# Strided attention on one core: output stores of every second SBUF row, 16 KiB each, from pairs of groups

## The chip, the core and the metric

The kernel runs on one core of a Trainium2 chip. The metric is the device time of one execution in microseconds (us). Each run was timed beside the kernel before on the same chip. The profile's span (127.6 us for the kernel before) is a little shorter than the timed 129.3 us; inside the profile, times are us from the start of the span. A run counts as slow when it is over 1.5% above the fastest of the same kernel.

## The reference

Every query of 8 x 12 heads, 1024 positions and 64 dimensions attends to the 16 keys at positions 0, 64, 128, ... (stride 64).

```python
attend_positions = np.arange(0, seq, stride)
...
scores = np.einsum('bhqd,bhkd->bhqk', q, k) * scale
weights = np.exp(scores - np.max(scores, axis=-1, keepdims=True))
weights = weights / (np.sum(weights, axis=-1, keepdims=True) + 1e-10)
result[:, :, i, :] = np.einsum('bhqk,bhkd->bhqd', weights, v)[:, :, 0, :]
```

Q (25.2 MB) must be read and the output (25.2 MB) written; the keys and values used are small. All is float32 in HBM.

## The kernel before

It works on 24 groups of four heads. A group is 1 MiB of Q and 1 MiB of output; in SBUF it has 128 rows of 8 KiB. Each group goes through a cast to bf16 (GpSimd), a transpose (VectorE), score and output matmuls (TensorE), an exponential (ScalarE), and a normalisation that writes the output tile. All transfers are issued from one queue (SyncE).

```python
    QBUFS = 8
    OBUFS = 9
...
    def load(g):
        qn[g] = qn_pool.tile([P, 32 * D], FP32, name="qn", tag="qn")
        n = P if g < 2 else 32
        _copy(nc, qn[g], _ap_with(Q, [[HG * SD // n, n], [1, HG * SD // n]], g * HG * SD))
...
    def store(g):
        o = out_sb[g]
        _copy(
            nc,
            _ap_with(out, [[16 * D, P], [2 * SD, 2], [1, 16 * D]], g * HG * SD),
            _ap_with(o, [o.ap[0], [1, 1], [1, 32 * D]]),
        )
...
    for g in range(NG):
...
        store(g)
        if g + QBUFS < NG:
            load(g + QBUFS)
```

A load reads 32 runs of 32 KiB (the first two loads read 128 runs of 8 KiB). A store reads 128 SBUF rows of 8 KiB and writes each as two pieces of 4 KiB that lie 512 KiB apart in HBM; the pieces of neighbouring rows lie side by side, so that a store fills two solid blocks of 512 KiB.

The softmax here doesn't subtract the row's maximum and nothing guards it: scores larger than these inputs give would overflow.

## Time and profile before

| | before |
|---|---|
| time, median of the six runs beside the changed kernel | 129.38 us |
| moved by DMA | 51.12 MB on the queue |
| share of the 16 DMA engines' time | 96.7% |
| busiest compute engine | VectorE, 75% |
| compute hands over the last group | 119.86 us |
| last store landed | 126.05 us |

"Landed" means that the trace shows the transfer as complete, and "the line" is the transfers issued and not yet landed. The two figures that fix the end are the last two rows: how late the compute is done, and how long the line of transfers before the DMA engines is at that moment. The profile lines are shown in the prediction.

### The profile page before, as it was taken

The page shows a single profiled execution, that of the slowest core. Times are in us where ns is not written, and L with a number is a line of the kernel's source. Part 1 is how long each engine was busy: PE and PEld are TensorE (multiplying, and loading weights), DVE is VectorE, ACT ScalarE, POOL GpSimd, SP SyncE. Part 2 cuts the span into 40 slices and gives each one's busy share as a digit, 9 for nine tenths or more (in the row PEclk, how much of TensorE's full clock was granted, in tenths as well). Part 3 has the DMA queues.
Part 4 walks back from the last instruction along what each step waited for, and adds up shares of the span by engine and source line. Part 5 has one row for each costly group of instructions (what it writes and reads, how often), then busy time and mean ns, then how long its engine had stood idle before and what let it go on. Part 6 is the DMA issues. An engine that isn't in the chain of part 4 may idle for free.

```text
span 127.6 us, 1150 instructions
## 1 busy us (share of the span) xinstructions
PE 67.2 (53%) x292; PEld 30.1 (24%) x292; DVE 95.5 (75%) x167; ACT 57.5 (45%) x96; POOL 90.3 (71%) x89
## 2 busy tenths in 40 slices
PE   0005267766456796436757565379734877365100
PEld 0002032233222343212423232124221433132000
DVE  6947557788898678898879888897889878977300
ACT  4110614576771458776445653543554626462100
POOL 8962489877898286898888888898689887433300
PEclk9999999999955558999756999955999657998555
DMA  2999989898998998999989989999999999999980
GB/s 68 378 319 468 462 360 483 349 483 362 460 465 352 480 455 339 506 385 393 501 344 447 460 375 450 426 403 457 442 380 455 439 393 421 424 426 424 429 360 26
DMA packets 7910, 51.19 MB, mean 401 GB/s; under 512 B 3872, under 2 KB 3872, under 8 KB 3872
## 3 DMA queue, kind: packets, MB, share of 16 engines
q1 hardware_dynamic: 7904, 51.12, 96.7%
q8 instruction: 2, 0.03, 0.1%
q14 instruction: 4, 0.03, 0.1%
HBM read 25.95 MB, written 25.17 MB: 401 GB/s over the span
## 4 chain that ended last, share of the span: by engine, by line
DVE 48%; DMA 16%; PE 14%; issue 9%; POOL 4%; SPq 1%; ACT 0%; DVEq 0%; POOLq 0%
DVE out_sb L245 30%; PE o_ps L235 11%; DVE qt L203 10%; DMA out_dram<-out_sb 9%; DMA qn<-in_Q_dram 7%; DVE rec L243 7%; PE sc L210 3%; POOL out_sb L248 2%; POOL qb L199 1%; DVE v_rep L184 1%; SPq L35 1%; POOL v L191 1%; ACT out_sb L247 0%; SPq L100 0%; DVE k_r L159 0%
## 5 line engine op out<-in xcount | busy, mean ns | idle before, releaser
L235 PE MATMUL o_ps<-v,w 128*128 128x260 bf16 x192 | 40.0, 333 | 36.1 <-DVE out_sb L245 34.5
L221 ACT ACTIVATE w<-sc 64x512 bf16<-64x512 f32 x48 | 35.3, 735 | 30.1 <-PE sc L210 28.3
L199 POOL CAST qb<-qn 128x2048 bf16<-128x2048 f32 x24 | 45.3, 1889 | 4.2 <-DMA qn<-in_Q_dram 4.2
L245 DVE TENSOR_TENSOR out_sb<-o_ps,rec 128x768 f32<-128x768 f32 x48 | 46.0, 958 | 1.7
L248 POOL TENSOR_TENSOR out_sb<-out_sb,rec 128x512 f32<-128x512 f32 x24 | 25.0, 1042 | 22.2 <-ACT out_sb L247 22.2
L210 PE MATMUL sc<-qt,k_t 128*128 128x512 bf16 x96 | 33.3, 479 | 12.8 <-DVE qt L203 11.6
L235 PEld LDWEIGHTS <-w 128*128 128x128 bf16 x192 | 18.7, 113 | 63.5 <-DVE out_sb L245 48.1
L203 DVE STREAM_TRANSPOSE qt<-qb 128x1024 int32<-128x1024 int32 x24 | 29.6, 1233 | 4.7 <-POOL qb L199 4.7
L243 DVE RECIPROCAL rec<-o_ps 128x12 f32<-128x12 f32 (+1 forms) x72 | 15.3, 212 | 15.9 <-PE o_ps L235 15.8
L247 ACT COPY out_sb<-o_ps 128x512 f32<-128x512 f32 x24 | 14.0, 585 | 24.9 <-DVE rec L243 12.1
L191 POOL TENSOR_TENSOR v<-mask,v_rep 128x256 bf16<-128x256 bf16 x24 | 16.0, 669 | 2.3 <-DVE v_rep L184 2.3
L210 PEld LDWEIGHTS <-k_t 128*128 128x128 bf16 x96 | 10.8, 113 | 23.8 <-issue 10.7
L169 ACT COPY k_t<-k_r 32x128 bf16<-32x128 bf16 x20 | 5.9, 295 | 2.2 <-DVE k_r L159 1.9
L129 POOL MEMSET k_t<- 128x4608 bf16 x1 | 3.9, 3937 | 0.0
L180 PE MATMUL vp<-v_bf,perm_v 128*128 128x384 bf16 x4 | 1.8, 513 | 2.4 <-DVE v_rep L184 2.4
L139 DVE TENSOR_SCALAR s_sel<-col,slot_f 128x4 bf16<-128x4 int16 x1 | 2.5, 2546 | 0.1
L158 ACT CAST k_bf<-k_raw 128x256 bf16<-128x256 f32 x3 | 1.2, 405 | 3.1 <-DMA k_raw<-in_K_dram 3.0
L184 DVE CAST v_rep<-vp 128x384 bf16<-128x384 f32 x4 | 2.1, 543 | 0.6 <-PE vp L180 0.6
L123 DVE MEMSET k_t<- 128x1152 uint32 x1 | 1.0, 1018 | 1.0 <-PEq L311 1.0
L158 ACT ACT_TABLE_LOAD x1 | 1.3, 1283 | 0.7 <-PEq L311 0.7
L127 DVE MEMSET w<- 128x512 uint32 x3 | 1.5, 485 | 0.2
L118 POOL COPY perm_v<-identity 128x32 bf16<-128x32 bf16 x8 | 1.2, 209 | 0.0
(16 smaller groups left out, 5.0 us busy)
## 6 DMA issues: line engine op xcount, KB each, us to landing
qn<-in_Q_dram SPq DMA_DIRECT2D x24, 1024.0 KB, 11.7
out_dram<-out_sb SPq DMA_DIRECT2D x24, 1024.0 KB, 9.8
k_raw<-in_K_dram SPq DMA_DIRECT2D x1, 384.0 KB, 4.3
v_raw<-in_V_dram SPq DMA_DIRECT2D x1, 384.0 KB, 7.3
```

Source lines behind the costliest of these rows:

```text
L129: nc.gpsimd.memset(k_t[:, 8:NG], 0.0)
L169: op(k_t[dst : dst + 32, 8 * m + c : 8 * m + 8 : 2, :, col : col + NK], k_r[src : src + 32, 4 * m : 4 * m + 4].rearrange("p n (a k f) -> p ...
L191: nc.gpsimd.tensor_tensor(out=vb[g][:, 0 : 4 * D].rearrange("p (s d) -> p s d", s=4), in0=mask, in1=v_rep[:, g // 2, g % 2].unsqueeze(1).t ...
L199: nc.gpsimd.tensor_copy(out=qb[g], in_=qn[g])
L203: nc.vector.transpose(qt[g].bitcast(I32), qb[g].bitcast(I32))
L210: nc.tensor.matmul(sc, lhsT=k_t[:, g, f, NK * (1 - e) : NK * (1 - e) + P], rhs=_ap_with(q, [q.ap[0], [D, 8], [16 * D, 2], [2, 32]], extra_ ...
L221: nc.scalar.activation(out=_ap_with(wa, [wa.ap[0], [P, 8], [1, 2], [2, 32]], extra_offset=64 * a), in_=sc[64 * a : 64 * a + 64].rearrange( ...
L235: nc.tensor.matmul(ps[:, i, 0 : 4 * D + 4], lhsT=wt[g][:, i0 + i], rhs=vb[g], start=True, stop=True,)
L243: nc.vector.reciprocal(r, ps[:, 0:n, 4 * D : 4 * D + 4])
L245: nc.vector.tensor_tensor(out=to, in0=o, in1=by, op=ALU.mult)
L247: nc.scalar.copy(to, o)
L248: nc.gpsimd.tensor_tensor(out=to, in0=to, in1=by, op=ALU.mult)
```

## The change

The intent is fewer and larger packets for the stores: 64 packets of 16 KiB for 1 MiB instead of 128 of 8 KiB. To have 16 KiB in a row, two groups share one output tile (a pair). A store takes every second row of it (rows 0, 2, 4, ... or 1, 3, 5, ...), so that a transfer still has 1 MiB and still touches all parts of SBUF. Between two such half stores goes one load. Ten Q buffers and four output pairs replace eight and nine.

```diff
-    QBUFS = 8
-    OBUFS = 9
+    QBUFS = 10
+    OBUFS = 4
...
-            out_sb[g] = out_pool.tile([P, 4, 8, D], FP32, name="out_sb", tag="out_sb")
+            if g % 2 == 0:
+                out_2[g // 2] = out_pool.tile(
+                    [P, 2, 4, 8, D], FP32, name="out_sb", tag="out_sb"
+                )
+            out_sb[g] = out_2[g // 2][:, g % 2]
...
-    def store(g):
-        o = out_sb[g]
+    def store(n, h):
+        o = out_2[n][h : P : 2]
         _copy(
             nc,
-            _ap_with(out, [[16 * D, P], [2 * SD, 2], [1, 16 * D]], g * HG * SD),
-            _ap_with(o, [o.ap[0], [1, 1], [1, 32 * D]]),
+            _ap_with(
+                out, [[32 * D, 64], [2 * SD, 4], [1, 16 * D]],
+                2 * n * HG * SD + h * 16 * D,
+            ),
+            _ap_with(o, [o.ap[0], [1, 1], [1, 64 * D]]),
         )
...
-        store(g)
-        if g + QBUFS < NG:
-            load(g + QBUFS)
+        if g % 2 == 1:
+            for h in range(2):
+                store(g // 2, h)
+                if g - 1 + h + QBUFS < NG:
+                    load(g - 1 + h + QBUFS)
```

More of the change, by code (lines that the diff above doesn't have):

```diff
@@ L184, in value_rows @@
             nc.vector.tensor_copy(out=v_rep[:, 6 * n : 6 * n + 6, c], in_=vp)
-    qb, qt, wt, vb, rec, out_sb = {}, {}, {}, {}, {}, {}
+    qb, qt, wt, vb, rec, out_sb, out_2 = {}, {}, {}, {}, {}, {}, {}
     def values(g):
```

## The prediction

> **What bounds the kernel now.** I read, in turn, the page's busy shares and DMA digits, the DMA queue's own waits with the landings, and the end of the timeline. First the page: busy us by engine, then DMA share and rate in 40 slices of 3.19 us, then the queue's packets, MB and share of the 16 DMA engines.
>
> ```profile
> PE 67.2 (53%) x292; PEld 30.1 (24%) x292; DVE 95.5 (75%) x167; ACT 57.5 (45%) x96; POOL 90.3 (71%) x89
> ...
> DMA  2999989898998998999989989999999999999980
> GB/s 68 378 319 468 462 360 483 349 483 362 460 465 352 480 455 339 506 385 393 501 344 447 460 375 450 426 403 457 442 380 455 439 393 421 424 426 424 429 360 26
> ...
> q1 hardware_dynamic: 7904, 51.12, 96.7%
> ```
>
> No compute engine is near full, but the one queue that carries every load and store is busy for 96.7% of its 16 engines' time and falls off only in the last two slices. (The ripple in GB/s comes from packets of 32 KiB being counted at one moment.) So the DMA engines never run dry. How long the line before them is, the DMA issues of two short windows tell (one store each, issued at 92.61 us and, the last of all, at 119.86 us; the last column is us from issue to landing):
>
> ```profile
> out_dram<-out_sb SPq DMA_DIRECT2D x1, 1024.0 KB, 16.0
> ```
>
> ```profile
> out_dram<-out_sb SPq DMA_DIRECT2D x1, 1024.0 KB, 6.2
> ```
>
> The landings in the trace form a strict first-in-first-out train: from 11.8 us on something lands every 2.4 to 2.5 us, to the last store at 126.05 us. At 92.6 us six transfers stand in line; at the end one.
>
> The compute is almost as long. What the issuing queue waited for, over the whole span:
>
> ```profile
> SPq L35 <- DVE out_sb L245: 83.0, 24, 11.3
> ```
>
> All 24 stores wait for VectorE's last normalisation of their group, none for a DMA. In the queue's timeline the stores go out every 4.1 to 4.4 us in the long middle, and the timeline of all engines ends so (start, duration, what):
>
> ```profile
> 118.55 0.23 DVE L243 RECIPROCAL rec<-o_ps 128x12 f32<-128x12 f32 x1 [0.81 <-PE o_ps L235]
> 118.82 0.96 DVE L245 TENSOR_TENSOR out_sb<-o_ps,rec 128x768 f32<-128x768 f32 x1
> 119.86 0.54 SPq L35 DMA_DIRECT2D out_dram<-out_sb  x1
> ```
>
> So two bounds lie within a few us of each other: a DMA train that is full from start to end, and a compute loop that hands over its last group at 119.86 us, when only one other store is left in line. Does compute wait for loads? Of GpSimd's waits, the casts of Q waited 4.2 us in 3 pieces: the first two are the ramp (7.66 and 11.84 us), the third, 0.79 us at 106.27, is absorbed before VectorE needs the result at 109.20. So compute is not held by the train in the steady part.
>
> **What the Trainium skill says.** (1) "DMA: Bandwidth & Descriptors", section "Why a DMA increments its semaphore by 16 and not by 1": a DMA is split over the largest k up to 16 that divides the slowest dimension of both sides. 64 rows give k = 16, four rows per engine, so a half store still uses all engines. No trace yet shows it for 64 rows; the 128-row stores have 128 packets, 8 per engine. (2) "SBUF — State Buffer", section "Door 1: The DMA port swizzle": partitions 0 to 63 reach only 8 of the 16 ports and moved 196 GB/s against 328 for all 128. That is why the change takes every second row: both halves then touch all 16 ports. It is also the main danger: whether two DMA engines meet on one port at the same moment depends on how rows are dealt to engines, which neither page nor trace tells for this shape. (3) The first page's section "Anatomy of one DMA" puts a fixed cost of about 2 us on a transfer, mostly completion. Here it is smaller: the first packet ran at 1.84 us for an issue at 0.73 us (1.1 us), and the last packet ended at 125.60 for a landing at 126.05 us (0.45 us); I use these 1.55 us.
>
> **The change, part by part.**
>
> *Bigger packets.* The packet records have a median of 311 ns for 8 KiB (stores) and 1219 ns for 32 KiB (loads). A straight line through both has 8.3 ns fixed per packet and 0.0369 ns per byte, so 16 KiB should take 614 ns (estimate). A store of 1 MiB is now 8 x 311 = 2.49 us per engine (landings: 2.50 us after the one before) and becomes 4 x 614 = 2.455 us. Saved: 0.033 us x 24 = 0.8 us of a train of 124 us. A load, at 2.40 to 2.44 us, does not change. This is all that the intent can give, even if the train alone set the end.
>
> *Ten Q buffers.* Ten loads go out before the first store. In before, the eighth load landed at 26.68 us and two more transfers at 29.15 and 31.58 us; now these two are loads, and the first stores go out at 27.36 us (group 1's time in before). The line is not empty until 31.6 us, so no hole opens. Every later load lands some two store times (5 us) earlier; only the 0.79 us wait at 106.27 goes, which cost nothing.
>
> *Four output pairs.* Pair n+4 needs pair n's two stores landed. Carrying the train forward at 2.44 us a load and 2.46 us a half store, pair 0 lands at 39 us and is wanted at 56 (just after group 7's store at 54.95), pair 5 at 88 against 97, pair 6 at 98 against 106, pair 7 at 105 against 114. The nearest margin is some 8 us, so no wait. The build's order shows the compute engines' instructions in the same order and number. The issue order shows eight semaphores in turn, so at most eight transfers in flight; the deepest point of my train (four issues together at 79.9 us with five in line) holds the last load back by about 0.5 us and leaves no hole.
>
> *The pairing at the end.* Group 22's store, which went out at 116.59 us and had landed by 123.62, now waits for group 23: 2 MiB go out together at 119.86 us. The train before it ends where group 21 landed in before, 121.16 us, less 22 x 0.033 = 0.7, so at about 120.4 us. The last pair's first packet can run at 119.86 + 1.1 = 120.97 us, two halves take 2 x 2.455 = 4.91 us, and the landing adds 0.45 us: 126.33 us, against 126.05. That is +0.3 us. The queue has one hole of about 1 us at 120 to 121 us, and the 0.8 us saved vanishes in it.
>
> Sum: 129.3 + 0.3 = 129.6 us.
>
> **The rivals.** (a) *The train alone sets the end*: then the saving of 0.8 us shows, 128.5 us. For it: 96.7% busy. Against it: the compute's hand-over at 119.86 us does not move, and behind it lie 2 MiB. (b) *Half stores collide on SBUF ports, or 4 KiB pieces at every second address are slow in HBM*. Neither is seen in the trace. If all stores ran at half rate, 24 x 2.45 = 59 us come on top, about 188 us; a fifth slower on the stores, 24 x 0.5 = 12 us, about 141 us. Against it: loads already write 128 rows from 32 packets and run at full rate, and choosing every second row looks aimed at just this. I give it 15%. (c) *Bursts*: two stores and two loads every 8.2 us instead of one each every 4.1 us. If the line ran dry between bursts it would cost up to 1 us each; but by my train four or five transfers are in line at each burst until 97 us. Then it thins: two at 105.16, one at 113.46 us (group 21's hand-over, where the first packet at 114.6 us meets a line that is free at about 115). A hole there costs 0.5 to 1 us: 130.5 us.
>
> **Range and chances.** Expected 129.6 us. Without (b) I see 128.5 to 130.6 us; the upper end is widened a little for thin lines and a slightly slow 16 KiB packet: 128.6 to 131.2 us. 2% is 2.6 us, so faster needs under 126.7 us, which would need the compute to hand over earlier: 2%. Slower needs over 131.9 us, in practice (b): 16%. Within: 82%.
>
> **What would show each step.** Stores: 1536 packets of 16 KiB at a median near 614 ns, 6368 packets on the queue. The last VectorE instruction at 119.8 us within 0.5 us; the last two stores issued together just after; a dip of the DMA digits near 120 us; the queue's waits still all on VectorE. Wrong would be: 16 KiB packets well above 640 ns (rival b), compute waiting for output buffers or Q loads, or a last VectorE instruction that moves by over 1 us, which I have no reason for.

## More of the kernel before

One line more is needed for the comparison: the DMA view of the kernel before between 30 and 50 us (packets, MB, mean rate), a stretch in which stores and loads alternate.

```profile
DMA packets 776, 8.44 MB, mean 422 GB/s; under 512 B 131, under 2 KB 131, under 8 KB 131
```

## The result, and the profile after

The changed kernel takes 135.74 us (median of six; 134.43 to 136.58, one of them slow), against 129.38 us. The ratio is 1.0467, with a 95% interval of 1.0413 to 1.0521. (A ratio here is the mean time of one kernel's fast runs over that of the other's fast runs of the same rounds, so it is not quite the ratio of the medians.) It is slower, and outside the predicted range of 128.6 to 131.2 us.

The page of the changed kernel, the lines that answer to those shown of before:

```profile
PE 69.2 (52%) x292; PEld 30.9 (23%) x292; DVE 95.7 (72%) x167; ACT 57.6 (43%) x96; POOL 90.4 (68%) x89
...
DMA  3999999999999999999999999999999999999981
GB/s 74 363 334 476 403 471 393 393 471 275 368 307 383 319 388 354 373 395 395 383 437 403 403 442 408 422 437 403 432 422 422 412 437 417 422 442 408 422 354 74
...
q1 hardware_dynamic: 6368, 51.12, 96.6%
```

The compute engines did the same work in the same busy time (VectorE 95.7 against 95.5 us). The packets fell to 6368, as predicted. The DMA engines are as busy as before, 96.6%, but over a span that is 5.9 us longer. So they were not idle more; they worked more slowly. Where, the GB/s digits show: from the tenth slice (30 us) on they are at 275 to 395 for eleven slices, and only in the second half, from the 21st on, back at 400 to 440. In the same stretch of 30 to 50 us as above:

```profile
DMA packets 432, 6.81 MB, mean 340 GB/s; under 512 B 112, under 2 KB 112, under 8 KB 112
```

That is 340 GB/s instead of 422. Between 108 and 121 us, where only stores are left, the same view has no loss at all; first before, then after:

```profile
DMA packets 757, 5.53 MB, mean 425 GB/s; under 512 B 82, under 2 KB 82, under 8 KB 82
```

```profile
DMA packets 422, 5.55 MB, mean 427 GB/s; under 512 B 83, under 2 KB 83, under 8 KB 83
```

The trace's packet records put a number on each store. A 16 KiB packet has a median of 616 ns over the whole run, which is what the prediction had set as the check, but the mean is 676 ns: the median hides the slow ones. Between 30 and 50 us the mean is 860 ns and 44% take over 900 ns. Sorted by start and cut into quarters (of the 64 packets of a half store, so in the first store about each engine's first, second, third and fourth), the first half store has means of 622, 779, 1184 and 1131 ns: it starts at full rate and falls to half. Such stores become milder from one to the next and are gone by about 80 us. Over the run an engine spends 64.9 us in store packets, against 59.8 us before: 5.1 us more. The 32 KiB load packets add 0.5 us (44 per engine, on the mean 1242 instead of 1230 ns). Together that is most of the 6.4 us by which the last landing is later, 132.46 against 126.05 us.

The queue's waits changed as well:

```profile
SPq L35 <- DVE out_sb L249: 68.2, 11, 15.4
SPq L35 <- DMA qn<-in_Q_dram: 11.9, 8, 2.0
SPq L335 <- DMA out_dram<-out_sb: 9.0, 1, 9.0
SPq L35 <- DMA out_dram<-out_sb: 7.0, 4, 2.5
```

The issuing queue now waits 18.9 us, in 12 pieces, for transfers to land, because eight semaphores allow eight transfers in flight (the completions in this trace fall on eight) and the line had reached that. These waits cost nothing by themselves: the line was full while they lasted. The last loads came late, though: GpSimd's casts waited 6.9 us for Q, in 5 pieces, against 4.2 us in 3 before. The compute handed over 2.1 us later:

```profile
120.96 0.96 DVE L249 TENSOR_TENSOR out_sb<-o_ps,rec 128x768 f32<-128x768 f32 x1
121.98 1.37 SPq L35 DMA_DIRECT2D out_dram<-out_sb  x2
```

Even so it is not the hand-over that sets the end. The two stores issued at 121.98 and 122.56 us land at 130.00 and 132.46 us, 8.0 and 9.9 us later, because others stood before them. The DMA line sets the end, and it is longer since its stores were slow.

### The profile page after: what moved, and what is told of

It reads as the page before. It is cut to its first block, busy times and chain, and to the rows that moved or that the text cites. A ratio compares the mean times of both kernels' runs of the same rounds, so it can differ in the third digit from the quotient of the medians.

```text
span 133.5 us, 1125 instructions
## 1 busy us (share of the span) xinstructions
PE 69.2 (52%) x292; PEld 30.9 (23%) x292; DVE 95.7 (72%) x167; ACT 57.6 (43%) x96; POOL 90.4 (68%) x89
## 3 DMA queue, kind: packets, MB, share of 16 engines
q1 hardware_dynamic: 6368, 51.12, 96.6%
HBM read 25.95 MB, written 25.17 MB: 383 GB/s over the span
## 4 chain that ended last, share of the span: by engine, by line
DMA 51%; DVE 13%; POOL 12%; PE 7%; issue 5%; SPq 2%; ACT 0%; POOLq 0%; DVEq 0%
DMA qn<-in_Q_dram 51%; POOL qb L199 7%; DVE out_sb L249 7%; PE o_ps L239 4%; DVE qt L203 4%; PE sc L210 3%; POOL out_sb L252 2%; POOL v L191 2%; DVE rec L247 2%; SPq L35 1%; ACT out_sb L251 0%; SPq L100 0%; DVE v_rep L184 0%; SPq L98 0%; DVE k_r L159 0%
## 5 line engine op out<-in xcount | busy, mean ns | idle before, releaser
L239 PE MATMUL o_ps<-v,w 128*128 128x260 bf16 x192 | 40.8, 340 | 36.0 <-DVE out_sb L249 34.5
L210 PE MATMUL sc<-qt,k_t 128*128 128x512 bf16 x96 | 35.1, 501 | 13.1 <-DVE qt L203 11.6
L239 PEld LDWEIGHTS <-w 128*128 128x128 bf16 x192 | 19.2, 116 | 64.0 <-DVE out_sb L249 48.0
```

The source lines that it names most:

```text
L210: nc.tensor.matmul(sc, lhsT=k_t[:, g, f, NK * (1 - e) : NK * (1 - e) + P], rhs=_ap_with(q, [q.ap[0], [D, 8], [16 * D, 2], [2, 32]], extra_ ...
L239: nc.tensor.matmul(ps[:, i, 0 : 4 * D + 4], lhsT=wt[g][:, i0 + i], rhs=vb[g], start=True, stop=True,)
```

## The experiments

What had to be explained: why are the early half stores slow, at up to twice the time, why not in the beginning of each store, and why does it wear off? Two theories stood at the start. *Theory S*: every second row makes two DMA engines meet on one SBUF port. *Theory H*: it is the HBM side, every second 4 KiB. All experiments are edits of the changed kernel's `store`, unless said otherwise, and all keep its ten Q buffers and output pairs. Those with a wrong result send right rows to wrong places, or compute with stale Q.

### First call: which side of the store

**e1, full rows of one group, as before**

```diff
-        o = out_2[n][h : P : 2]
+        o = out_2[n][:, h]
-                out, [[32 * D, 64], [2 * SD, 4], [1, 16 * D]],
-                2 * n * HG * SD + h * 16 * D,
+                out, [[16 * D, P], [2 * SD, 2], [1, 16 * D]],
+                (2 * n + h) * HG * SD,
```

> The changed kernel with its pairing, its ten Q buffers, its four output pairs and its order of issues, but each store takes all 128 rows of one group, 8 KiB a row, as before. If the half store itself is slow (either of the two theories below), this is back at the time predicted from the order alone, 129 to 130.5 us, with 8 KiB packets at 311 ns. If the order and the bursts cost the 6.4 us, it stays at 134 to 136.5 us.

Measured: correct, 129.15 us (129.00 to 129.42), ratio 0.9982 (0.9951 to 1.0014). Packets at 311 ns throughout. So buffers and the pair tile are not the cause; the shape of the half store is. One weakness: here the first store of a pair can go out when its own group is done, so the run doesn't test two stores issued together. The next one does.

**e2, every second SBUF row, but HBM without holes** (wrong result)

```diff
-                out, [[32 * D, 64], [2 * SD, 4], [1, 16 * D]],
-                2 * n * HG * SD + h * 16 * D,
+                out, [[16 * D, 64], [SD, 4], [1, 16 * D]],
+                (2 * n + h) * HG * SD,
```

> Wrong result on purpose. SBUF side as in the changed kernel (every second row, 16 KiB), but a half store writes 1 MiB of HBM without holes: 4 KiB pieces of neighbouring rows lie side by side. Theory S (two DMA engines meet on one SBUF port because of every second row): still slow, 134 to 136.5 us, first 16 KiB packets of the early stores up to 1.2 us. Theory H (every second 4 KiB of HBM is slow to write): 129 to 130.5 us, all 16 KiB packets near 616 ns.

Measured: 130.14 us (129.61 to 130.80), ratio 1.0059 (1.0006 to 1.0112). Packets of 30 to 50 us have a mean of 642 ns, and only 4% take over 900 ns (in the last quarter of the very first store). This is what the prediction had in mind for the whole change, pairing at the end included.

**e3, full SBUF rows, but every second 4 KiB of HBM** (wrong result)

```diff
-        o = out_2[n][h : P : 2]
+        o = out_2[n][:, h]
-                out, [[32 * D, 64], [2 * SD, 4], [1, 16 * D]],
+                out, [[32 * D, P], [4 * SD, 2], [1, 16 * D]],
```

> Wrong result on purpose. HBM side of the changed kernel (each store fills every second 4 KiB of 2 MiB), SBUF side as before (128 rows of 8 KiB). Theory S: 129 to 130.5 us, packets at 311 ns. Theory H: slow, 134 us or more, 8 KiB packets well over 311 ns in the early stores.

Measured: 137.16 us (134.95 to 138.96; two of the four are slow, the two fast ones have 134.95 and 135.71). The profile, of a fast run, repeats the changed kernel's pattern with packets of half the size: the first store's quarters are 314, 372, 634 and 560 ns, and it wears off in the same way. Theory S is out: SBUF rows are those of before, and the slowness is all there. The three DMA views between 31.5 and 34 us, within the first half store, of the changed kernel, of e2 and of e3:

```profile
DMA packets 38, 0.62 MB, mean 249 GB/s; under 512 B 1, under 2 KB 1, under 8 KB 1
```

```profile
DMA packets 64, 1.05 MB, mean 419 GB/s; under 512 B 16, under 2 KB 16, under 8 KB 16
```

```profile
DMA packets 77, 0.65 MB, mean 259 GB/s; under 512 B 1, under 2 KB 1, under 8 KB 1
```

**e4, rows 0 to 63 and 64 to 127 as halves** (right result)

```diff
-        o = out_2[n][h : P : 2]
+        o = out_2[n][64 * h : 64 * h + 64]
-                2 * n * HG * SD + h * 16 * D,
+                2 * n * HG * SD + h * SD,
-                out, [[32 * D, 64], [2 * SD, 4], [1, 16 * D]],
+                out, [[16 * D, 64], [2 * SD, 4], [1, 16 * D]],
```

> Right result. A half store takes rows 0 to 63 or 64 to 127 instead of every second row; its HBM side has no holes between rows. Theory S with ports as the limit: half of the ports for each store, so stores take up to 4.9 us instead of 2.46 and the time goes to 150 to 190 us. Theory H: 129 to 130.5 us, as nothing lies at every second 4 KiB.

Measured: 141.56 us median of 135.70, 141.11, 142.02 and 142.04; the profiled run is a slow one (142.02), so I draw nothing from its size. Even the one fast run, 135.70 us, lies about 6 us above the kernel before. The time lies under what theory S expected and above theory H's.

### Second call: step, size of the holes, ports, packets

e3's slowness wears off, and in the records the engines drift apart while it does: in the changed kernel the share of time in which at least 13 of the 16 engines are in store packets falls from 52% (30 to 45 us) to 2% (75 to 90 us). In e1, which is never slow, it stays above 35% in both stretches. This suggested that the loss needs the engines in step.

**e6, half of the engines made to lag by one load before the first store** (right result)

```diff
     def load(g):
         qn[g] = qn_pool.tile([P, 32 * D], FP32, name="qn", tag="qn")
+        if g == QBUFS - 1:
+            for first, rows, k in ((0, 32, 8), (32, 32, 8), (64, 64, 16)):
+                _copy(
+                    nc, qn[g][first : first + rows],
+                    _ap_with(Q, [[rows * 32 * D // k, k], [1, rows * 32 * D // k]],
+                             g * HG * SD + first * 32 * D),
+                )
+            return
```

> Right result. The changed kernel, but the last load before the first store is split so that half of it (2 pieces of 8 shares) runs on 8 of the 16 DMA engines alone; these 8 then lag by about one load, 2.4 us, when the first half store starts. Theory H with relief by spread (a half store is slow only while nearly all 16 engines write the same half at once): the early 16 KiB packets run near 616 to 680 ns from the first store on, and the time is 130 to 132 us (the 129.6 of the order alone, plus about 1.2 us that the lagging engines end later). If the spread of the engines has nothing to do with it and something else wears off: early packets up to 1.2 us as before, 134 to 137 us.

Measured: correct, 131.25 us (131.07 to 131.40), ratio 1.0134 (1.0107 to 1.0160). For 75% of the time from 31 to 101 us eight engines store while eight load, give or take one (86% from 31 to 60 us). Only the first store still has a slow quarter (617, 862, 618, 616 ns); from the second on all quarters are at 611 to 639. Between 30 and 50 us the rate is back from 340 to 392 GB/s:

```profile
DMA packets 480, 7.84 MB, mean 392 GB/s; under 512 B 120, under 2 KB 120, under 8 KB 120
```

One load, cut differently, takes away most of the loss without touching a store. That step matters is thus shown, not inferred.

**e7, every second 8 KiB** and **e8, every second 16 KiB** (wrong results; e8 ran in the third call)

```diff
-        o = out_2[n][h : P : 2]
+        o = out_2[n][:, h]
-                out, [[32 * D, 64], [2 * SD, 4], [1, 16 * D]],
-                2 * n * HG * SD + h * 16 * D,
+                out, [[64 * D, P], [16 * D, 2], [1, 16 * D]],      # e7
+                2 * n * HG * SD + h * 32 * D,
+                out, [[128 * D, 64], [16 * D, 4], [1, 16 * D]],    # e8
+                2 * n * HG * SD + h * 64 * D,
```

> Wrong result on purpose. As the run with every second 4 KiB of HBM and 128 SBUF rows, but every second 8 KiB, still in pieces of 4 KiB. If it is the address bit of 4 KiB alone (half of something in HBM is then left out), both values occur now and it is fast: 129 to 130.5 us, 8 KiB packets at 311 ns. If any alternation does it: 134 us or more, early packets at up to 630 ns.

> Wrong result on purpose. As the run with every second 8 KiB, but every second 16 KiB (four pieces of 4 KiB side by side, then a hole of 16 KiB). If 4 KiB is the only size that matters: 129 to 130.5 us and 311 ns. If the address bit of 16 KiB selects something as well: 134 us or more.

Measured: e7 129.36 us (ratio 0.9990, 0.9964 to 1.0015), e8 129.14 us (0.9961, 0.9931 to 0.9991), packets at 311 ns in both. Holes of 8 or 16 KiB do no harm; holes of 4 KiB do.

**e9, rows 0 to 63 and 64 to 127, HBM without holes** (wrong result)

```diff
-        o = out_2[n][h : P : 2]
+        o = out_2[n][64 * h : 64 * h + 64]
-                out, [[32 * D, 64], [2 * SD, 4], [1, 16 * D]],
-                2 * n * HG * SD + h * 16 * D,
+                out, [[16 * D, 64], [SD, 4], [1, 16 * D]],
+                (2 * n + h) * HG * SD,
```

> Wrong result on purpose. SBUF side of the run with rows 0 to 63 and 64 to 127, HBM side without any holes (1 MiB in a piece). If that run was slow for its SBUF rows (half of the ports): 135 to 142 us again, and slow packets in the early and the last stores. If for its HBM side (every second 256 KiB): 129 to 130.5 us and 616 ns.

Measured: 138.23 us (137.09 to 140.62, the last a slow run), ratio 1.0644 (1.0600 to 1.0688), with a fast profile. The first store's quarters are 623, 718, 1082 and 1440 ns, and the last three stores are slow again (2.9 to 3.2 us per engine instead of 2.46). So e4's rows are a second, separate trouble, on the SBUF side, and the choice of every second row does avoid it. It, too, is mild while stores and loads overlap (612 to 690 ns in the quarters between 60 and 105 us), and the first three stores after the last load are at full rate as well (2.46 to 2.50 us per engine). Why the last ones are slow again is not shown.

**e5, one store of 2 MiB, all 128 rows of 16 KiB; the last pair as two stores** (right result)

```diff
-        o = out_2[n][h : P : 2]
+        if n < NC - 1:
+            if h == 1:
+                return
+            o = out_2[n]
+            _copy(nc, _ap_with(out, [[16 * D, P], [2 * SD, 4], [1, 16 * D]], 2 * n * HG * SD),
+                  _ap_with(o, [o.ap[0], [1, 1], [1, 64 * D]]))
+            return
+        o = out_2[n][:, h]
+        # then the store of e1
```

> Right result. The intent without the half stores: one store of 2 MiB takes all 128 rows of a pair, 16 KiB each; the last pair goes out as two stores of one group. Theory H: nothing is left out in HBM, so 16 KiB packets run at 614 to 616 ns throughout, the train is up to 0.8 us shorter, and the time is 128.5 to 130 us. If a 16 KiB packet is itself the trouble: 134 us or more.

Measured: correct, 129.85 us (129.20 to 130.92), ratio 1.0037 (0.9996 to 1.0079). In quarters of a store the 16 KiB packets run at 614 to 625 ns, except in the last quarter of the first store (730 ns). The packet size is not the trouble, and it is no gain either.

### Third to fifth call: what stands behind the store

**e10, even and odd places of 4 KiB mixed within a store** (wrong result; edit of e3)

```diff
-                out, [[32 * D, P], [4 * SD, 2], [1, 16 * D]],
+                out, [[32 * D, P], [4 * SD + (1 - 2 * h) * 16 * D, 2], [1, 16 * D]],
```

> Wrong result on purpose. The run with every second 4 KiB of HBM and 128 SBUF rows (134.95 us at best), with one thing changed: of a row's two 4 KiB pieces the first goes to an even place and the second to an odd one (the other way about in the other half). Row pitch, holes, piece size and packets stay. Theory H as the address bit of 4 KiB: both values occur in every store, so it is fast, 129 to 130.5 us, early 8 KiB packets near 311 ns. If the holes or the pitch of 8 KiB are what is slow: 134 us or more, early packets at up to 630 ns.

Measured: 153.94 us (152.38 to 155.93; two of the four are slow), which fits neither. The time has a dull cause: in this build the second store of a pair has a wait for the first one to land (12 waits for stores, 92.7 us in all). The packets are of more use. Every first store is at 309 to 315 ns, the very first included, where e3 had 634. But every second store of the mixed phase is slow in its second half (for example 329, 314, 410, 580 ns). So mixing even and odd places is not a full cure.

**e11, no load after the first ten** (wrong result)

```diff
                 if g - 1 + h + QBUFS < NG:
-                    load(g - 1 + h + QBUFS)
+                    qn[g - 1 + h + QBUFS] = qn[(g - 1 + h) % QBUFS]
```

> Wrong result on purpose. The changed kernel with its half stores, but no load after the first ten: later groups take the Q of an earlier one from SBUF. So stores have the DMA engines to themselves, and the engines start each pair of halves together after an idle stretch. If half stores are slow by their HBM addresses alone whenever all 16 engines write the same half together: packets of the later halves up to 1.2 us in every pair, to the end. If it takes loads from HBM beside the stores: all 16 KiB packets near 616 ns. The time is then the compute's, 127 to 131 us, and decides nothing.

Measured: 129.65 us (two runs). No packet is above 758 ns between 30 and 50 us, and the mean is 622, with the engines in step in every pair: 16 packets start within 0.14 to 0.16 us in nearly every store. The first half store of this kernel is the same instruction on the same data after the same ten loads as in the changed kernel. There it fell to 249 GB/s between 31.5 and 34 us; here the DMA view of the same stretch is:

```profile
DMA packets 80, 1.05 MB, mean 419 GB/s; under 512 B 16, under 2 KB 16, under 8 KB 16
```

The one difference is what stands in line behind it: a half store here, a load there. My theory H, that the addresses of the writes alone are slow, fell with this run.

**e12, every third 4 KiB of a 3 MiB region** (wrong result; edit of e3)

```diff
-                out, [[32 * D, P], [4 * SD, 2], [1, 16 * D]],
-                2 * n * HG * SD + h * 16 * D,
+                out, [[48 * D, P], [6 * SD, 2], [1, 16 * D]],
+                (2 * n + h) // 3 * 12 * SD + (2 * n + h) % 3 * 16 * D,
```

> Wrong result on purpose. 128 SBUF rows of 8 KiB; a store fills every third 4 KiB of 3 MiB instead of every second of 2 MiB (three groups share a region). There are more holes, but even and odd places of 4 KiB alternate from row to row. If what counts is that all pieces of a store have the same address bit of 4 KiB: fast, 129 to 130.5 us, early packets near 311 ns. If holes of 4 KiB as such are slow: 134 us or more, early packets at up to 630 ns.

Measured: 129.31 us (128.92 to 129.37), ratio 0.9978 (0.9932 to 1.0025), 311 ns. Holes of 8 KiB between single 4 KiB pieces do no harm where even and odd places alternate from row to row. Of all HBM patterns tried in a running line (e4 and e9, with their SBUF rows, aside), only those with every piece of the store at an even place, or every one at an odd place, were badly slow.

**e13, both half stores side by side, then both loads** (right result)

```diff
             for h in range(2):
                 store(g // 2, h)
-                if g - 1 + h + QBUFS < NG:
+            for h in range(2):
+                if g - 1 + h + QBUFS < NG:
                     load(g - 1 + h + QBUFS)
```

> Right result. The changed kernel with both half stores of a pair side by side and both loads after them. If a half store is slowed by a load directly behind it on all engines: first halves at 616 ns throughout, second halves of the early pairs up to 1.2 us a packet; about half of the 6.4 us is lost, 131.5 to 133.5 us. If loads anywhere in the mix do it: both halves slow, 134 to 137 us.

Measured: correct, 134.09 us (133.91 to 134.84), ratio 1.0357 (1.0316 to 1.0398). The time is a little above the range I gave, but the packets are as sharp as could be wished. The first halves of all pairs are at 615 to 622 ns (one quarter at 641). The second halves of the first four pairs have 1203, 1199, 1048 and 755 ns in their third quarter. In the changed kernel both halves have a load behind them and both are slow; here only the second half has one, and only the second half is slow. In the DMA views, first 31.5 to 34 us (mostly the first half), then 34 to 36.5 us (the second half, with a load behind it):

```profile
DMA packets 80, 1.05 MB, mean 419 GB/s; under 512 B 16, under 2 KB 16, under 8 KB 16
```

```profile
DMA packets 40, 0.66 MB, mean 262 GB/s; under 512 B 3, under 2 KB 3, under 8 KB 3
```

Less than half of the loss is saved (1.7 us of 6.4): fewer stores are slow, but the ones that are lose as much as before.

**e14, later loads copied from a tile in SBUF** (wrong result)

```diff
+    q_keep = const.tile([P, 32 * D], FP32, name="q_keep")
...
-                    load(g - 1 + h + QBUFS)
+                    sbuf_load(g - 1 + h + QBUFS)     # _copy(nc, qn[g], q_keep)
```

> Wrong result on purpose. The changed kernel with its order of halves and loads, but every load after the first ten copies 1 MiB from a tile in SBUF instead of HBM (that tile takes one load more at the start, about 2.4 us). If it is the load's HBM read that collides with the half store's HBM writes: 16 KiB packets near 616 ns from the first store on. If any transfer behind a half store does it, without HBM reads: early packets up to 1.2 us as in the changed kernel. The time decides nothing.

Measured: the early half stores stay at 612 to 643 ns; their mean between 30 and 50 us is 621. A transfer stands behind each of them, as in the changed kernel, but it does not read HBM (the run reads 12.32 MB of HBM, the changed kernel 25.95). So the mere presence of another transfer is not enough, and a read of HBM is what is missing. One more thing differs, though: the copy comes in 128 packets of 8 KiB where the load has 32 of 32 KiB, and no run separates the two. (The time, 134.1 us with one load more at the start, was not meant to decide.)

**e15, the two forms of e10 exchanged** and **e16, dense stores in e10's position** (wrong results; edits of e10 and of e1)

```diff
         o = out_2[n][:, h]
+        h = 1 - h                                     # e15
...
-                (2 * n + h) * HG * SD,
+                (2 * n + h) * HG * SD - h * 16 * D,   # e16: overlaps, so that it must wait
```

> Wrong result on purpose. The run with even and odd places mixed in each store, with the forms of the first and the second half exchanged; as there, the second half waits for the first to land, so the time is long (150 to 156 us) and decides nothing. If the slow packets there belonged to the place (second half, which starts after the queue ran dry, all engines in step): the second halves are slow again, and the first ones at 310 ns. If they belonged to the form (odd first, then even): now the first halves are slow and the second ones fast.

> Wrong result on purpose (the second store of a pair lies 4 KiB lower, so that it overlaps the first one's last piece and has to wait for it). Stores are those of before, 128 full rows and no holes, but the second one of a pair starts on an empty queue, all engines in step, with a load behind it, as in e10 and e15. If the place in HBM is a condition: 8 KiB packets near 311 ns in second stores too. If tight step and a load behind are enough: second stores of the early pairs slow in their second half, 400 to 620 ns, as in e10 and e15. The time is long in both cases, 145 to 156 us, by the wait.

Measured: e15 155.01 us, e16 153.09 us. In both, first stores have 309 to 315 ns and second stores are slow again (e15: 328, 314, 403, 596; e16: 328, 314, 448, 608 in the first pair, and 361 to 611 ns in the last quarter of the six after it). So the slowness in e10 went with the position, not with the form. And in this position even the dense stores of before are slow: the line before them has just run short (in e16 the engines stood idle for 0.07 to 0.93 us on the mean around the start of these stores), and a load is issued right behind. Tighter step alone does not tell them apart: in e16 their first 16 packets start within 0.32 us, but so do those of e8's first stores, in a running line with a load behind, at 311 to 315 ns. Late in these runs, where no loads are left, stores start within 0.14 to 0.31 us and are near full rate.

## Why the prediction was wrong

**What held.** The packet itself: 614 ns were estimated for 16 KiB and the median is 616. The 6368 packets, four per engine on all 16 engines for a half store, the compute engines' busy times, the order of issues, no hole after the first ten loads, and no wait of the compute for an output pair are all as predicted. The sum for the order and the pairing, 129.6 us, is close to e2's 130.14, which has the changed kernel's SBUF rows, pairing, order and packets, but no holes in HBM.

**The step that failed** is the one called "Bigger packets": "A store of 1 MiB ... becomes 4 x 614 = 2.455 us. Saved: 0.033 us x 24 = 0.8 us". The early stores took 3.7 us of each engine's time (622 + 779 + 1184 + 1131 ns), and all stores together cost 5.1 us more where 0.8 us less had been summed. I took a packet's duration from a trace in which stores were never in trouble and carried it over to a new pattern of addresses.

**A rival named the place and was dismissed for a wrong reason.** Rival (b) had "4 KiB pieces at every second address are slow in HBM" beside colliding SBUF ports, with 15%. Against it stood that loads run at full rate and that every second row looked aimed at avoiding ports. Both are arguments about SBUF; neither says anything about where the writes land. e2 and e3 each change one side only and show that the SBUF side is nearly innocent (e2) and the HBM side is enough (e3). The rival's size was off too, as it charged all 24 stores alike, while the loss wears off.

**What the runs showed in its place** are three conditions, each with a run that takes it away. (1) All pieces of the store lie at even, or all at odd, places of 4 KiB: without it, e2, e7, e8 and e12 are within 1% of before. (2) A load stands directly behind the store: without it, e11 has no slow stores (no quarter of one is over 665 ns), and in e13 only the halves with a load behind them are slow. That it is the load's read of HBM rests on e14 alone, whose copies also have smaller packets. (3) The 16 engines are in step: with half of them lagging, e6 gets back 4.5 us of the 6.4 (135.74 to 131.25). The third fits the wearing off: an engine that is held up falls behind the others, and so each slow store would spread the engines, until most of the time some write while others read. In the changed kernel the first 16 packets of a store start within 0.62 us in the first store and within 2.21 us in the sixth; that the slow stores cause this spread is inferred.

How can a load that comes later slow a store? The Trainium skill, "DMA: Bandwidth & Descriptors", section "Two DMAs through the same engine are not ordered", states that descriptors "*start* in order but are pipelined, and the engine's read and write sides are separate queues". Then the read side may already fetch the next load while the store's writes are still under way. This agrees with the slow packets being those of a store's second half, and with e11 and e13. That the reads run ahead is my inference; no record here shows a read apart from its write.

**The hand-over and the rival (a).** I had the compute's hand-over at 119.86 us set the end, with a hole in the queue at 120 us. With slower stores the line was never empty, the last loads came later, the hand-over moved to 121.98 us (the last VectorE instruction ended at 121.92 us, not at the predicted 119.8), and the train set the end. So rival (a) was right about what bounds it, with the sign of its saving reversed.

**What stays open.** Which property of HBM makes even-only or odd-only pieces suffer from a load behind them is not known; no run here looks inside it. Condition (1) is also not absolute: the first dense stores of e2 and e5 are slow at their end (897 and 730 ns in the last quarter), and in e16 dense stores suffered more, after the line had run short. So a store with a load behind can be slow in other patterns too; what makes it so there was not found, as tighter step does not tell e16 from e8. Whether it is the load's read of HBM or its larger packets that (2) needs was not separated either.

None of the versions beats the kernel before clearly: e1 is the best with a right result, at a ratio of 0.9982, within noise. The half store's packets are worth under 1 us, and the compute's hand-over and the train end within a few us of each other, so that either alone gives little.

## What to carry to other kernels

When a transfer's shape changes, ask for both of its ends: a row choice that is good for SBUF can leave a comb in HBM. A packet's duration holds for the pattern and the neighbours it was measured with; check the new pattern with one run that changes only that side. If a DMA-bound kernel slows in one phase and recovers later, look at whether the engines go in step, and at which transfer stands behind the slow one.

## What the Trainium skill lacked or had wrong

- "DMA: Bandwidth & Descriptors" has slow HBM patterns only for large power-of-two row pitches (section "Latency and other measured facts"). It lacks this one: stores of 4 KiB pieces at every second 4 KiB, with an HBM load directly behind, ran at about 250 GB/s instead of 419 (31.5 to 34 us, against e2 and e11), while every second 8 or 16 KiB and every third 4 KiB do no harm.
- No page says that a store's rate depends on the transfer behind it. The same half store ran at 622, 779, 1184 and 1131 ns in its quarters with a load behind and at 615 to 625 with a store behind.
- No page shows by a measurement that it matters whether the 16 DMA engines go in step; the first page's entry on row pitches only infers an aliasing of "lock-stepped per-partition streams". Here letting eight engines lag by one load gave back 4.5 us. That a load of 8 shares uses 8 engines, as that page's section "Why a DMA increments its semaphore by 16 and not by 1" has it, agrees with the 8 and 8 that the records show afterwards.
- "SBUF — State Buffer", section "Door 1: The DMA port swizzle", gives rows 0 to 63 some 60% of the rate of all 128 rows (196 against 328 GB/s). Here (e9) such half stores were slow at the start and in the last stores (2.9 to 3.2 us per engine instead of 2.46); from 60 to 105 us they ran near full rate, 612 to 690 ns a packet against 616. The page measures one transfer, and two at a time on the two halves; it lacks half-row stores in a long line with loads of all rows.
- The fixed cost of about 2 us in the first page's section "Anatomy of one DMA — SWDGE (gpsimd) path" is that of transfers issued from GpSimd. For this kernel's SyncE queue it is a little lower: 1.1 us from issue to the first packet and 0.45 us from the last packet to the landing in the kernel before; in e11 a store issued on an idle queue lands 4.2 to 4.4 us after its issue, of which 2.5 us are packets, so 1.7 to 1.9 us.
